# Attention's half-tile moves issued by GpSimd instead of SyncE, and the up weights' sums begun 45 instead of 55 planned microseconds apart

## The chip, the core and the metric

One core of a Trainium2 chip. The metric is the device time of one execution in microseconds (us), the median of several; lower is better. The engines that matter are TensorE (PE, with its weight loads as PEld), VectorE (DVE), ScalarE (ACT), GpSimd (POOL) and SyncE (SP). SP computes nothing; it issues DMAs. ACT and POOL can issue DMAs too, from their own streams of instructions. Every engine executes its stream in order.

## What is computed

One layer on x of 1024 tokens by 1024 features, all in float32: a mixer (attention of 8 heads of 64 features with three dilations, beside 4 mLSTM heads of 128) and a gated feed-forward of width 2816 with a short convolution.

```python
h = h + _hybrid_mixer(_rmsnorm(h, mixer_norm_w[layer]), w_in[layer], ...)
h = h + _conv_ffn(_rmsnorm(h, ffn_norm_w[layer]), w_ffn_up[layer], ...)
return _rmsnorm(h, final_norm_w)

s = jnp.einsum('nbqhd,nbkhd->nbhqk', qb, kk) * (Dh ** -0.5)      # scores of a head
u = _causal_dwconv(h @ w_ffn_up, ffn_conv_w, ffn_conv_b)         # up projection
```

## The kernel before, in words

**Precision by splitting.** Most operands are cut into a high part and a remainder of float32r type, and a product is made of three matmuls (`mm3`). The remainder of a weight tile (`w15l`, `w16l`, ...) is subtracted on POOL or DVE.

**Heads.** The features of x times a head's query and key columns come out of PE as one tile `t`: queries in partitions 0 to 63 (`lo`), keys in 64 to 127 (`up`). `stacks(h, ps)` (line 912) scales it, makes the high part `q1` (`copy`, ACT or DVE) and the remainder `q2` (DVE), and then needs three stacked tiles: `kS` holds the key's remainder over the key's high part, `q1` the query's high part over the query's remainder, `q2` the remainder over the high part. The halves change partitions, so four DMAs of 64 x 1024 floats (256 KB each) move them (lines 931 to 934). The first pair writes `kS` out of `q2` and `q1`. The second pair overwrites the upper halves of `q1` and `q2`, which the first pair has read, so it waits until the first pair has landed. `scores()` (line 943) multiplies `q1` and `q2` with `kS`: 24 matmuls a head, eight heads in order, h0 to h7. In the trace all eight heads' tiles are called `q` and `kS`.

**Sums of weights.** The feed-forward's products use Strassen's seven products in place of eight, for which sums of weight quarters are made in DRAM by `sums` (line 788): a plain copy issued by ACT (line 799), then an add into the same place issued by POOL with `accum_op` (line 796), four times in turn for the up weights (`usum`, 5632 KB each) and four times for the down weights (`tsum`). An add waits until the copy into its place has landed. They stand at lines 804 and 806; the first reader of `usum` is the feed-forward's load, at 589 us in the trace.

**What sets the order.** The program is written out by hand-made lanes (generators), each of which stops at a `yield need(...)`. A planner (`Clock`, line 30) keeps an estimated time for each engine (`clk.eng`), for each tile's readiness (`clk.wr`) and last use (`clk.acc`). `Lanes.run` (line 184) always goes on with the lane of the lowest priority number whose need is met by PE's planned time. So an estimate changes the order of the instructions in the streams, and nothing else: on the chip real semaphores decide. `sums(70, 55, ...)` means: the first step is put into its stream when PE's planned time passes 70, the next at 125, then 180, and so on to 455; odd steps are copies on ACT, even ones adds on POOL. `move` (line 306) issues on SP's queue and advances the planner's `dma` clock. `scores` is put into PE's stream when `q1`, `q2` and `kS` are ready by plan.

**SP's queue.** SP also issues all loads and stores (`dma`, line 291, and `store`, line 1441), in program order with the moves.

Of the kernel before, what the change touches and what calls it, by code (L numbers as in the profile page):

```python
# [217 lines left out]
def need(*tiles, pg=0, bk=0, cond=None, keep=0, kb=0):  # L218

    return tiles, pg, bk, cond, keep, kb  # L220
# [3 lines left out]
def tile_hybrid_layer(ctx, tc, xT, x, w_t, w_v, w_g, w_o, w_uq, w_dq, params, fnw, c_id, c_att, c_sel,  # L224
                      c_rst, c_tri, out):
    nc = tc.nc
    clk = Clock()
# [3 lines left out]
    pool = Engine(clk, nc.gpsimd, "pool")  # L231
# [7 lines left out]
    usum = {p: dram.tile([DFF, 512], F32, name=f"usum{p}") for p in (3, 5, 6, 7)}  # L239
# [8 lines left out]
    def page(name, dt=F32):  # L248
        slot[0] = freep.pop(0)
        t = pages.tile([128, PGW], dt, tag="pg", name=name)  # L250
        clk.floor[t.tensor.name] = slot[0]
        return t

    def free(*ts):
        for t in ts:
            freep.append(clk.last(t))
# [10 lines left out]
    def freebank(t):  # L267
        freeb.append(t)
# [19 lines left out]
    lanes = Lanes(clk, when)  # L288
# [14 lines left out]
    def f32(ap):  # L303
        return ap.bitcast(F32)

    def move(dst, src):

        nc.sync.dma_start(f32(dst), f32(src))
        t = max(clk.eng.get("dma", 1.7), clk.ready(src), clk.last(dst))
        clk.eng["dma"] = t + 0.7  # L310
        for a in (dst, src):
            n = a.tensor.name
            clk.acc[n] = max(clk.acc.get(n, 0.0), clk.eng["dma"] + 2.0)
        for k in clk.cells(dst):
            clk.wr[k] = clk.eng["dma"] + 2.0
            clk.weng[k] = "dma"

    def copy(out_, in_, scale=None):

        if clk.eng.get("act", 0.0) <= clk.eng.get("dve", 0.0):  # L320
            act.activation(out_, in_, AF.Copy, **({} if scale is None else {"scale": scale}))
        elif scale is None:
            dve.tensor_copy(out_, in_)
        else:
            dve.tensor_scalar(out_, in_, scale, None, op0=OP.mult)
# [10 lines left out]
    class Feed:  # L336
# [54 lines left out]
        def put(self, whl):  # L391
            for hi, lo in whl:
                free(hi, lo)
# [11 lines left out]
    for o in order.split():  # L405
        n = int(o[1])
# [171 lines left out]
    def fin_ready(ps, hf):  # L578

        if hf < len(ps) and "R" in flags:  # L580
            return max(clk.ready(ps[hf]), 1e-9)
        return False
# [65 lines left out]
    def project():  # L648

        for n, (kind, arg) in enumerate(plan):  # L650
# [7 lines left out]
            if kind in ("ml", "att"):  # L658
                (wh, wl), = whl
                ps = []  # L660
                for hf in range(2):
                    yield wneed(whl, bk=1, kb=FGB - 1 if "R" in flags else 1)
                    p = bank("fg")
                    if hf == 0:
                        lanes.add(ml_conv(arg, ps) if kind == "ml" else stacks(arg, ps), 3)
                    for k in range(8):
                        ks = slice(k * 128, (k + 1) * 128)
                        mm3(p, wh[:, ks], wl[:, ks], xh[k][:, H[hf]], xl[k][:, H[hf]], k == 0, k == 7)
                        yield need()
                    ps.append(p)  # L670
# [117 lines left out]
    def sums(t, dt, quarters, into, order):  # L788


        flat = lambda a: a.rearrange("(r c) n -> r (c n)", c=4)
        for to, src, add in order:
            yield need(cond=lambda: clk.eng.get("pe", 0.0) > t)
            src = flat(quarters[src] if isinstance(src, tuple) else into[src])
            if add:
                nc.gpsimd.dma_start(flat(into[to]), src, accum_op=OP.add, max_dma_last_dim=8192)
                clk.eng["pool"] = clk.eng.get("pool", 0.0) + 1.5
            else:
                nc.scalar.dma_start(flat(into[to]), src)
            t += dt  # L800

    uq = {(i, j): w_uq[i, j] for i in range(2) for j in range(2)}
    dq = {(i, j): w_dq[i, j] for i in range(2) for j in range(2)}
    lanes.add(sums(70, 55, uq, usum, ((5, (1, 0), 0), (5, (1, 1), 1), (6, 5, 0), (6, (0, 0), 1), (3, 6, 0),
                                      (3, (0, 1), 1), (7, (1, 0), 0), (7, (0, 0), 1))), 0.5)
    lanes.add(sums(530, 45, dq, tsum, ((5, (0, 0), 0), (5, (0, 1), 1), (6, 5, 0), (6, (1, 1), 1), (4, 6, 0),
                                       (4, (1, 0), 1), (7, (0, 1), 0), (7, (1, 1), 1))), 0.6)
# [104 lines left out]
    def stacks(h, ps):  # L912
        for hf in range(2):
            yield need(pg=0 if hf else 4, keep=2, cond=lambda: fin_ready(ps, hf))
            if hf == 0:
                t = page("t")
            dve.tensor_mul(t[:, H[hf]], ps[hf], R[:, H[hf]])
            freebank(ps[hf])
        if h == 7:
            free(R)  # L920
        yield need(t, pg=3)
        q1 = page("q1", F32R)
        q2 = page("q2", F32R)
        kS = page("kS", F32R)
        lo, up = slice(0, 64), slice(64, 128)
        A = slice(0, S)
        copy(q1[:, A], t[:, A])
        yield need(q1)
        dve.tensor_sub(q2[:, A], t[:, A], f32(q1[:, A]))
        yield need(q2)  # L930
        move(kS[lo, A], q2[up, A])
        move(kS[up, A], q1[up, A])
        move(q1[up, A], q2[lo, A])
        move(q2[up, A], q1[lo, A])
        free(t)
        den = small.tile([128, 8], F32, name="aden", bufs=4)
        heads[h] = (q1, q2, kS, den)
# [761 lines left out]
```

## Time and profile before

| what | us |
|---|---|
| median of 3 runs | 1254.02 |
| lowest and highest run | 1248.43, 1255.01 |
| profiled execution, its own time | 1251.1 |
| its span | 1249.3 |
| PE busy | 1221.0 (98%) |
| DVE, ACT, POOL busy | 868.2, 576.5, 300.0 |
| mean granted share of PE's clock | 0.99 |

Busy time says how long an engine had work, not whether it set the end. Here PE is busy nearly all the time, so what counts is the few places where PE waits, what released it, and at which clock it ran.

### The profile page before, as it was taken

What the parts mean: (1) busy time and instruction counts of PE and PEld (TensorE: products, weight loads), DVE (VectorE), ACT (ScalarE), POOL (GpSimd) and SP (SyncE); (2) the same over time, 40 slices, a digit from 0 to 9 for tenths busy, and PEclk for the clock granted to TensorE, in tenths of its full rate; (3) what the DMA queues carried; (4) which work ended last, traced back from release to release, by engine and by line L of the source; (5) the groups of instructions that cost most, each with busy time, mean ns of one, the idle gap of its engine ahead of it and who ended that gap; (6) DMA issues with size and microseconds to landing.
All of it is one profiled execution on the core that took longest, in us unless ns stands there. A gap on an engine that the chain in (4) does not pass through costs nothing. (4 is left out here: it accounts for less than half of the span.)

```text
span 1249.3 us, 17498 instructions
## 1 busy us (share of the span) xinstructions
PE 1221.0 (98%) x6366; PEld 1031.3 (83%) x6366; DVE 868.2 (69%) x1622; ACT 576.5 (46%) x1146; POOL 300.0 (24%) x213
## 2 busy tenths in 40 slices
PE   9999999999999699999999999999999999999997
PEld 6899898988998598788878888888888888888886
DVE  6733472657784487635799877777776878877865
ACT  4454554536562366334654344343343444343553
POOL 3420132121103103121133332323322222424002
PEclk9999999999999799999999999999999999999999
DMA  9460656668493759823663865546634279433334
GB/s 332 174 213 25 147 163 231 144 152 251 129 193 94 269 178 233 214 86 142 143 212 133 243 222 164 188 161 195 179 107 152 82 288 409 148 102 90 97 97 147
DMA packets 66366, 216.41 MB, mean 173 GB/s; under 512 B 7268, under 2 KB 8804, under 8 KB 61288
## 3 DMA queue, kind: packets, MB, share of 16 engines
q1 hardware_dynamic: 61032, 146.09, 34.8%
q0 software_dynamic: 4352, 34.60, 13.7%
q10 hardware_dynamic: 896, 34.60, 8.1%
q8 instruction: 50, 0.82, 0.3%
q14 instruction: 36, 0.29, 0.1%
HBM read 182.76 MB, written 93.32 MB: 221 GB/s over the span
## 5 line engine op out<-in xcount | busy, mean ns | idle before, releaser
L153 PE MATMUL bank<-xb,W 128*128 128x512 f32 x1848 | 431.1, 395 | 2.6 <-POOL W L153 2.1
L153 PEld LDWEIGHTS bank<-xb,W 128*128 128x128 f32 x1848 | 347.8, 188 | 84.9 <-POOL W L153 2.5
L153 PE MATMUL bank<-B,A 128*128 128x512 f32 x924 | 214.0, 394 | 0.0
L153 PEld LDWEIGHTS bank<-B,A 128*128 128x128 f32 x924 | 173.6, 188 | 40.2
L153 POOL TENSOR_TENSOR W<-ur,W 128x512 fp32r<-128x512 f32 x82 | 107.2, 1329 | 278.4 <-ACT W L153 258.0
L153 ACT ACTIVATE ua<-bank,pr 128x512 f32<-128x512 f32 x84 | 63.0, 777 | 168.9 <-DVE bank L153 161.0
L153 DVE SCALAR_TENSOR_TENSOR ua<-bank,pr,ua 128x511 f32<-128x511 f32 (+1 forms) x168 | 125.4, 746 | 15.9 <-ACT ua L153 12.9
L153 DVE TENSOR_TENSOR bank<-bank,ut 128x512 f32<-128x512 f32 x84 | 58.6, 697 | 38.2 <-PE bank L153 37.2
L153 ACT ACTIVATE W<-ur 128x512 fp32r<-128x512 f32 x133 | 78.5, 623 | 5.9 <-DMA ur<-in_w_uq_dram 3.2
L153 ACT ACTIVATE A<-g 128x512 fp32r<-128x512 f32 x76 | 47.3, 627 | 71.9 <-DVE g L153 47.2
L153 DVE CUSTOM_DVE_ANT_0 P<-bank,matt 128x512 f32<-128x512 f32 (+3 forms) x96 | 50.7, 552 | 19.6 <-PE bank L153 17.5
L153 ACT ACTIVATE P<-P,nmx 128x128 f32<-128x128 f32 (+3 forms) x64 | 49.5, 773 | 29.3 <-DVE nmx L153 29.0
L153 DVE TENSOR_TENSOR ut<-ut,bank 128x512 f32<-128x512 f32 x66 | 45.0, 681 | 19.5 <-PE bank L153 19.0
L153 DVE TENSOR_TENSOR B<-br,B 128x512 fp32r<-128x512 f32 x67 | 50.4, 755 | 11.5 <-ACT B L153 11.4
L153 DVE TENSOR_TENSOR PT<-bank,PT 128x512 fp32r<-128x512 f32 (+1 forms) x80 | 48.3, 630 | 8.2 <-ACT PT L153 7.9
L153 PE MATMUL bank<-kS,q 128*128 128x512 f32 (+3 forms) x192 | 42.4, 354 | 10.9 <-DMA q<-q 10.9
L153 POOL TENSOR_TENSOR A<-g,A 128x512 fp32r<-128x512 f32 x17 | 23.2, 1372 | 122.2 <-ACT A L153 122.2
L153 DVE TENSOR_TENSOR W<-ur,W 128x512 fp32r<-128x512 f32 x72 | 49.9, 701 | 2.2 <-ACT W L153 1.5
L153 DVE TENSOR_TENSOR A<-g,A 128x512 fp32r<-128x512 f32 x60 | 41.7, 700 | 13.6 <-ACT A L153 13.2
L153 DVE TENSOR_TENSOR hq<-hq,bank 128x512 f32<-128x512 f32 x56 | 34.9, 681 | 20.9 <-PE bank L153 20.9
L153 ACT ACTIVATE B<-br 128x512 fp32r<-128x512 f32 x69 | 42.4, 619 | 14.9 <-DMA br<-in_w_dq_dram 10.1
L153 ACT ACTIVATE PT<-bank 128x512 fp32r<-128x512 f32 (+1 forms) x71 | 36.5, 547 | 24.9 <-PE bank L153 23.4
(357 smaller groups left out, 2467.2 us busy)
## 6 DMA issues: line engine op xcount, KB each, us to landing
usum<-in_w_uq_dram POOLq DMA_DIRECT2D x4, 5632.0 KB, 34.9
ur<-usum SPq DMA_DIRECT2D x88, 256.0 KB, 4.5
ur<-in_w_uq_dram SPq DMA_DIRECT2D x66, 256.0 KB, 4.6
usum<-in_w_uq_dram ACTq DMA_DIRECT2D x2, 5632.0 KB, 21.1
usum<-usum ACTq DMA_DIRECT2D x2, 5632.0 KB, 22.8
tsum<-in_w_dq_dram POOLq DMA_DIRECT2D x4, 2816.0 KB, 18.1
gp<-ua SPq DMA_DIRECT2D x22, 512.0 KB, 2.9
g<-gp SPq DMA_DIRECT2D x22, 512.0 KB, 7.6
```

The costliest lines, as they stand in the source:

```text
L153: r = f(*a, **k)
```

## The change

The moves go from SP's queue to POOL's: `put` takes the place of `move`, issues by `nc.gpsimd.dma_start`, and advances the planner's `pool` clock by 1.0 a move instead of the `dma` clock by 0.7. The planner counts a move as landed 4.0 after its start (before: 2.7). Between the first pair and the second stands a new `yield need(kS)`: the second pair is put into the stream only when PE's planned time has reached `kS`'s planned landing, and other lanes may go on meanwhile. The steps of the up weights' sums are begun at planned times 70, 115, 160, 205, 250, 295, 340 and 385 instead of 70, 125, 180, 235, 290, 345, 400 and 455. The down weights' sums stay.

```diff
-    def move(dst, src):
-
-        nc.sync.dma_start(f32(dst), f32(src))
-        t = max(clk.eng.get("dma", 1.7), clk.ready(src), clk.last(dst))
-        clk.eng["dma"] = t + 0.7
+    def put(dst, src):
+
+        nc.gpsimd.dma_start(dst, src)
+        t = max(clk.eng.get("pool", 0.0), clk.ready(src), clk.last(dst))
+        clk.eng["pool"] = t + 1.0
         for a in (dst, src):
             n = a.tensor.name
-            clk.acc[n] = max(clk.acc.get(n, 0.0), clk.eng["dma"] + 2.0)
-        for k in clk.cells(dst):
-            clk.wr[k] = clk.eng["dma"] + 2.0
-            clk.weng[k] = "dma"
+            clk.acc[n] = max(clk.acc.get(n, 0.0), t + 4.0)
+        if dst.tensor.name in clk.floor:
+            for k in clk.cells(dst):
+                clk.wr[k] = t + 4.0
+                clk.weng[k] = "dma"
...
-    lanes.add(sums(70, 55, uq, usum, ((5, (1, 0), 0), (5, (1, 1), 1), (6, 5, 0), (6, (0, 0), 1), (3, 6, 0),
+    lanes.add(sums(70, 45, uq, usum, ((5, (1, 0), 0), (5, (1, 1), 1), (6, 5, 0), (6, (0, 0), 1), (3, 6, 0),
                                       (3, (0, 1), 1), (7, (1, 0), 0), (7, (0, 0), 1))), 0.5)
...
-        move(kS[lo, A], q2[up, A])
-        move(kS[up, A], q1[up, A])
-        move(q1[up, A], q2[lo, A])
-        move(q2[up, A], q1[lo, A])
+        put(f32(kS[lo, A]), f32(q2[up, A]))
+        put(f32(kS[up, A]), f32(q1[up, A]))
+        yield need(kS)
+        put(f32(q1[up, A]), f32(q2[lo, A]))
+        put(f32(q2[up, A]), f32(q1[lo, A]))
```

## Rows read from the trace of the kernel before

**Rows 1.** The page: the span, and busy time with its share by engine.
```profile
span 1249.3 us, 17498 instructions
PE 1221.0 (98%) x6366; PEld 1031.3 (83%) x6366; DVE 868.2 (69%) x1622; ACT 576.5 (46%) x1146; POOL 300.0 (24%) x213
```
**Rows 2.** PE's waits, whole span: waiting <- released by: total us, times, longest.
```profile
PE bank L153 <- DMA q<-q: 10.9, 2, 8.9
```
**Rows 3.** Timeline of PE, 410 to 442: start, us, instructions, [idle before <- releaser].
```profile
417.70 1.14 PE L153 MATMUL bank<-kS,q 128*128 128x512 f32 x4
427.74 0.48 PE L153 MATMUL bank<-kS,q 128*128 128x128 f32 x1 [8.89 <-DMA q<-q]
430.22 1.65 PE L153 MATMUL bank<-kS,q 128*128 128x128 f32 x5 [2.00 <-DMA q<-q]
431.67 0.63 PE L153 MATMUL bank<-xh,w17h 128*128 128x512 f32 x1
...
435.34 0.39 PE L153 MATMUL bank<-xl,w17h 128*128 128x512 f32 x1
```
**Rows 4.** Timeline of SP's queue: moves of h2 (first pair), h4 (first), h5 (both).
```profile
312.31 3.75 SPq L308 DMA_DIRECT2D kS<-q x2
...
393.63 1.10 SPq L308 DMA_DIRECT2D kS<-q x2
...
403.54 1.11 SPq L308 DMA_DIRECT2D kS<-q x2
411.53 1.10 SPq L308 DMA_DIRECT2D q<-q x2
```
**Rows 5.** DMA issues at 393, 403 and 411: count, KB each, median us to landing.
```profile
kS<-q SPq DMA_DIRECT2D x2, 256.0 KB, 3.2
kS<-q SPq DMA_DIRECT2D x2, 256.0 KB, 7.3
q<-q SPq DMA_DIRECT2D x2, 256.0 KB, 16.2
```
**Rows 6.** Tile usum: issue ns, first and last start; then landings, issues at 345, 408, 480.
```profile
L796 POOL DMA_DIRECT2D usum<-in_w_uq_dram x4: 1132/1172/1291, 133.4 to 480.4; - x4
L799 ACTq DMA_DIRECT2D usum<-in_w_uq_dram x2: 503/552/602, 72.0 to 408.3; - x2
L799 ACTq DMA_DIRECT2D usum<-usum x2: 477/485/493, 184.9 to 296.9; - x2
...
usum<-in_w_uq_dram POOLq DMA_DIRECT2D x1, 5632.0 KB, 32.1
usum<-in_w_uq_dram ACTq DMA_DIRECT2D x1, 5632.0 KB, 21.0
usum<-in_w_uq_dram POOLq DMA_DIRECT2D x1, 5632.0 KB, 38.8
```
**Rows 7.** DMA queues between 411 and 427: packets, MB, share of 16 engines.
```profile
q10 hardware_dynamic: 115, 5.05, 88.4%
q1 hardware_dynamic: 92, 0.32, 5.4%
```
**Rows 8.** Page: the one queue of DMAs that POOL issues, packets, MB, share.
```profile
q0 software_dynamic: 4352, 34.60, 13.7%
```
**Rows 9.** DMA issues of the first 17 us, queue q1: 64 KB loads, ahead and behind.
```profile
w0r<-in_w_t_dram SPq DMA_DIRECT2D x6, 64.0 KB, 2.3
...
ident<-in_c_id_dram SPq DMA_DIRECT2D x1, 64.0 KB, 5.5
```
**Rows 10.** Timeline of POOL, 376 to 412.
```profile
384.12 2.92 POOL L153 TENSOR_TENSOR adn<-ams,ahp 128x16 f32<-128x16 f32 x1 [4.23 <-DVE ams L153]
387.03 2.42 POOL L153 TENSOR_TENSOR w17l<-wr,w17h 128x1024 fp32r<-128x1024 f32 x1
```
**Rows 11.** Timeline of PE: first score matmuls of h2 and of h4.
```profile
329.92 0.62 PE L153 MATMUL bank<-kS,q 128*128 128x128 f32 x4
...
403.71 1.57 PE L153 MATMUL bank<-kS,q 128*128 128x128 f32 x9
```

## The prediction, made before the changed kernel was run

> **What bounds the kernel now.** I read the page first: PE is busy 1221.0 of 1249.3 us [rows 1], so the end is set by PE, and a change can only move the time through PE's waits, its clock, or the amount of its work. The work doesn't change. The list of PE's waits came next: the only one of any size that a DMA ends is the one on `q<-q`, attention's second pair of moves, 10.9 us in two pieces [rows 2]. No wait of PE for a weight load is in that list, so what stands behind the moves on SP's queue costs nothing today.
>
> The timeline of PE shows the place. The scores of h5 should begin when the matmuls of 417.70 end, at 418.84; they begin at 427.74 and 430.22 [rows 3]. After that idle time a 128x512 matmul takes 0.63 us up to 435 and 0.39 from there on [rows 3], that is PE at the lower of its two clock levels (1.2 GHz) and then at the higher one (2.4). From 430.2 to 435.1 that costs about half of 4.9 us, 2.4 us. So this one stall is worth 10.9 + 2.4 = 13.3 us.
>
> Why it is there: h5's second pair was issued at 411.53 [rows 4] and took 16.2 us to land, where a pair on quiet queues takes 3.2 [rows 5]. A 5632 KB copy for the sums had been issued by ACT at 408.3 and landed 21.0 us later [rows 6]. Between 411 and 427 the copy's queue q10 moved 5.05 MB and SP's queue q1 0.32 [rows 7]. Moves and sums share the DMA engines, and the moves lose.
>
> **The change part by part.**
>
> *The copies go away from h5.* The planned times of the four copies were 70, 180, 290, 400, and they were issued at 72.0, 184.9, 296.9 and 408.3 [rows 6]: planned time plus 2.0, 4.9, 6.9, 8.3. The last copy is now planned at 340, so about 347.5 real, and lands at 347.5 + 21.0 = 368.5. h5's moves (403 to 412) find no copy: the stall of 13.3 us goes. What is late next there is the following part.
>
> *The adds come under the moves.* The adds were planned at 125, 235, 345, 455 and are now at 115, 205, 295, 385. One lasts 32.1 to 38.8 us [rows 6]; I take 35. The old ones were in flight at 133 to 167, 228 to 265, 345 to 377 and 480 to 519, beside no pair of moves but, just, h7's. The new third one runs at about 292 to 337, the new fourth at about 391 to 426. For the fourth: planned 385 is about 393 in real time by the offset above, but POOL can run ahead of PE as far as its own work lets it, and its stream is busy until 387.03 + 2.42 = 389.45 [rows 10]. I take 391, with 380 and 396 as ends. h4's first pair of moves is ready at 393.63 [rows 4].
>
> *The moves join the adds' queue.* All that POOL issues is in one queue, q0: its 34.60 MB are those of the eight adds alone [rows 8]. From now on the moves stand in it behind the adds. No row shows two DMAs in q0 at once, so I bound the wait. Lower bound: q0's DMAs don't hold each other up, and a move takes the 3.2 us of a quiet pair [rows 5]. Upper bound: a move starts when the add ahead of it is through. The nearest row for order inside one queue is q1 at the start: a 64 KB load lands 2.3 us after issue, and one of the same size issued behind half a megabyte and more of other loads of that queue 5.5 us after [rows 9]. That is the nearer kin, so I take the upper bound. The Trainium skill says the same in words: on its page "DMA: Bandwidth & Descriptors", section "Queues, rings and completion order", each engine consumes the descriptors of one ring in order, while different rings take turns by packet; and by the section "SWDGE vs HWDGE vs iDMA" only one queue is allocated for DMAs issued by GpSimd. By that rule moves behind an add wait for all of it; the trace of before shows neither for q0.
>
> *The price for h4.* The add issued at 391 lands at 426. h4's first pair lands with it, at about 426.5. POOL then issues the second pair: an add's issue costs POOL 1.13 to 1.29 us [rows 6], a move's on SP 0.55 (1.10 for two [rows 4]); I take 1.0 each, so 2. Landing takes 3.2 to 3.5 more: `q1` and `q2` are ready at 432. PE reaches h4's scores at 403.71 in the trace of before [rows 11]; the planner now counts about 10 us for the four moves instead of 6.8, so it fills in some 3 us of other matmuls first: 407. Stall: 432 - 407 = 25 us. After it the clock is low for about as long as in rows 3, 2.4 us. Sum +27.4. With the add issued at 380 and landing in 32.1 it is 412 + 5.5 - 407 = 11 us; with 396 and 38.8 it is 33 us. It hardly matters on which side of h4's first pair the add falls in POOL's stream: if the add comes between the pairs, the second pair waits for it instead, and h4 is ready at 396 + 35 + 1 = 432 again. If it comes behind all four, h5's moves of 403.54 wait in its place.
>
> *h2.* The third add, issued between 291 (when POOL has issued h1's moves) and 302, lands between 326 and 337. h2's first pair (312.31 [rows 4]) lands then, its second 5.5 us later, at 331.5 to 342.5. h2's scores begin at 329.92 [rows 11] and now about 333: between 0 and 9.5 us, I take 2, since POOL tends to be early. h3, h0, h1 have either slack or no add beside them: 0.
>
> *POOL's own time.* 32 issues at 1.0 us are 32 us on an engine that is busy 300.0 of 1249.3 [rows 1]. Behind a waiting second pair stand weight remainders (like `w17l`, 2.42 us [rows 10]) and the small `adn`. They are made one unit ahead of use, and between 250 and 520 us PE's list of waits has none on them; I take 0, and up to 3 us if h4's wait holds one up that isn't covered by PE's own stall.
>
> *SP freed.* SP no longer stops at moves; loads are issued earlier. PE waits for none of them: 0.
>
> *Sum*, against the profiled execution's 1251.1 us: -13.3 + 27.4 + 2 = +16.1, 1267. That execution lies 2.9 below the median of the runs, 1254.0; on the median the sum gives 1270. I forecast 1269.
>
> **The rivals.**
>
> *Moves aren't held behind an add (faster).* If q0 lets a move through in its usual time, or if the order shifts so that the moves of h4 and h5 fall outside the adds, the old stall is gone and nothing replaces it: -13.3, 1241. It decides at one point: whether a move issued during an add lands in some 3 to 6 us or with the add. For it: no row contradicts it, and packets of two different queues do mix in the trace (q1 moved its 0.32 MB beside q10 [rows 7]). Against it: rows 9, and that the two windows of 10 to 12 planned us of h4 and h5 both lie within 35 us of planned 385, so a dodge needs a shift of the plan of over 20 us. Chance 0.25.
>
> *One stall for another (no change).* The stall of h4 comes out at about 13 us and only replaces h5's: the add must have landed by about 414, thus been issued by 379 to 382. POOL would have to issue it ahead of `adn`, for which it waits 4.23 us before 384.12 [rows 10]; that is possible if the planner sets it there. Time 1250 to 1258. Chance 0.10.
>
> *The forecast, slower.* 1259 to 1282, chance 0.65.
>
> **How the numbers follow.** Over 0.5%, about what a measurement of this kernel can tell from no change, is 6.3 us. Slower 0.65, same 0.10, faster 0.25. The slower case's own range is 1259 (stall 15) to 1282 (stall 33, h2 5). To leave out no more than 2 in 10 the range must reach into the faster case: I take 1240 to 1282, which leaves out about half of that case and the tail above.
>
> **What would show it.** In the profile after: PE's waits should have a stall of 20 to 30 us on the moves (`DMA q<-q` or `kS`) once, near 407 to 432, with PE's clock at 1.2 GHz behind it; the stall at 418 to 430 should be gone; moves issued by POOL during an add should show a landing time of 15 to 35 us, others 3 to 5; POOL should wait long for `kS<-q` in front of a second pair. If moves during an add land within 6 us, the queue step is wrong and the time will be near 1241. If no add is in flight when h4's and h5's moves go, the planned offsets were wrong. If a stall is there but PE waits for a `w..l` tile, POOL's queue was the price.

## The result, and the profile after

The changed kernel takes 1272.88 us (median of 4 runs, 1270.92 to 1273.61) beside 1251.94 of the kernel before on the same chip: 1.0166 times as long, 95% interval 1.0132 to 1.0200. The forecast was 1269, slower.

The page of the profile after. The answers to [rows 1] and [rows 8]:

```profile
span 1271.8 us, 17500 instructions
PE 1221.9 (96%) x6366; PEld 1032.0 (81%) x6366; DVE 865.1 (68%) x1616; ACT 580.4 (46%) x1152; POOL 315.7 (25%) x245
...
q0 software_dynamic: 6912, 42.99, 16.2%
```

PE's busy time is nearly the same, 1221.9 us over as many instructions; the 22.5 us that the span grew are PE's waiting and its lower clock. q0 grew from 34.60 to 42.99 MB: the 32 moves joined the eight adds. PE's waits, the answer to [rows 2] (waiting <- released by: total us, times, longest):

```profile
PE bank L153 <- DMA q<-q: 34.5, 4, 17.5
PE bank L153 <- POOL W L153: 2.0, 1, 2.0
```

The wait on the moves grew from 10.9 to 34.5 us. The timeline of PE shows it at two places, and none at h5 any more (the answer to [rows 3]):

```profile
321.74 0.62 PE L153 MATMUL bank<-kS,q 128*128 128x512 f32 x2
339.55 0.44 PE L153 MATMUL bank<-kS,q 128*128 128x128 f32 x1 [15.55 <-DMA q<-q]
340.75 2.50 PE L153 MATMUL bank<-kS,q 128*128 128x128 f32 x7 [0.75 <-DMA q<-q]
...
448.84 0.45 PE L153 MATMUL bank<-kS,q 128*128 128x128 f32 x1 [17.49 <-DMA q<-q]
450.01 0.98 PE L153 MATMUL bank<-kS,q 128*128 128x128 f32 x3 [0.72 <-DMA q<-q]
```

The first is h2 (16.3 us), the second h4 (18.2 us). The timeline of POOL tells why, the answer to [rows 4] and [rows 10]:

```profile
300.22 1.06 POOL L308 DMA_DIRECT2D q<-q  x2
301.27 1.23 POOL L797 DMA_DIRECT2D usum<-in_w_uq_dram  x1
302.01 1.54 POOL L308 DMA_DIRECT2D kS<-q  x2
336.58 1.02 POOL L308 DMA_DIRECT2D q<-q  x2 [33.02 <-issue]
...
413.17 1.11 POOL L308 DMA_DIRECT2D kS<-q  x2 [4.58 <-issue]
414.27 1.23 POOL L797 DMA_DIRECT2D usum<-in_w_uq_dram  x1
...
419.75 1.50 POOL L308 DMA_DIRECT2D q<-q  x2
```

Around 301 the third add goes out right ahead of h2's first pair, and POOL then sits idle for 33 us before it issues the second pair ("issue" says that the profile names no releaser; the first pair, for which it must wait, has landed at 335.5 by the rows below). Around 414 the fourth add falls between h4's two pairs. The landing times, the answer to [rows 5] and [rows 6], of what was issued between 300 and 303, then at 413, then at 419 (count, KB, median us to landing):

```profile
usum<-in_w_uq_dram POOLq DMA_DIRECT2D x1, 5632.0 KB, 33.6
q<-q POOLq DMA_DIRECT2D x2, 256.0 KB, 3.5
kS<-q POOLq DMA_DIRECT2D x2, 256.0 KB, 33.5
...
kS<-q POOLq DMA_DIRECT2D x2, 256.0 KB, 3.2
...
q<-q POOLq DMA_DIRECT2D x2, 256.0 KB, 29.3
```

Moves issued one us ahead of an add land in 3.5 and 3.2 us, as on SP before. Moves issued behind it land in 33.5 and 29.3, with the add. What the DMA engines did meanwhile says whether the moves were slow or not begun. All packets between 306 and 326, then the table of queues there, then all packets between 336 and 338, when h2's second pair of moves runs alone:

```profile
DMA packets 513, 4.21 MB, mean 211 GB/s; under 512 B 0, under 2 KB 0, under 8 KB 0
...
q0 software_dynamic: 512, 4.19, 102.0%
...
DMA packets 22, 0.09 MB, mean 45 GB/s; under 512 B 0, under 2 KB 0, under 8 KB 22
```

A move's packets are smaller than 8 KB. In these 20 of the 33 us for which h2's first pair stood in q0 behind the add, not one packet under 8 KB was moved. The pair was not slow, it had not begun.

### The profile page after: what moved, and what is told of

Read it like the earlier page. It is cut to its first block, busy times and chain, and to the rows that moved or that the text cites. A ratio compares the mean times of both kernels' runs of the same rounds, so it can differ in the third digit from the quotient of the medians.

```text
span 1271.8 us, 17500 instructions
## 1 busy us (share of the span) xinstructions
PE 1221.9 (96%) x6366; PEld 1032.0 (81%) x6366; DVE 865.1 (68%) x1616; ACT 580.4 (46%) x1152; POOL 315.7 (25%) x245
## 3 DMA queue, kind: packets, MB, share of 16 engines
q0 software_dynamic: 6912, 42.99, 16.2%
q10 hardware_dynamic: 896, 34.60, 8.2%
## 5 line engine op out<-in xcount | busy, mean ns | idle before, releaser
L153 DVE SCALAR_TENSOR_TENSOR ua<-bank,pr,ua 128x511 f32<-128x511 f32 (+1 forms) x168 | 125.3, 746 | 16.1 <-ACT ua L153 12.9
L153 DVE TENSOR_TENSOR bank<-bank,ut 128x512 f32<-128x512 f32 x84 | 58.5, 697 | 30.0 <-PE bank L153 28.8
L153 PE MATMUL bank<-kS,q 128*128 128x512 f32 (+3 forms) x192 | 43.1, 357 | 34.5 <-DMA q<-q 34.5
L153 PEld LDWEIGHTS bank<-kS,q 128*128 128x128 f32 x192 | 32.8, 197 | 39.0 <-issue 34.7
L153 DVE TENSOR_TENSOR W<-ur,W 128x512 fp32r<-128x512 f32 x72 | 50.0, 701 | 13.8 <-ACT W L153 13.2
L153 ACT ACTIVATE B<-br 128x512 fp32r<-128x512 f32 x69 | 42.4, 620 | 16.0 <-DMA br<-in_w_dq_dram 11.1
```

Of the source, the lines that this page charges most:

```text
L153: r = f(*a, **k)
```

## The experiments

Three theories were kept apart. **A**: a move waits in GpSimd's queue until the add ahead of it is through. **B**: the adds take the DMA engines, so a move beside an add is slow in any queue. **C**: the new order of the streams, the later second pair or the issue by GpSimd costs the time by itself. Ratios are against the kernel before on the same chip.

| run | what | us (median) | ratio, 95% interval |
|---|---|---|---|
| sp_queue | changed, moves issued by SP | 1260.13 | 1.0073, 1.0049 to 1.0097 |
| moves_only | changed, sums 55 apart | 1248.90 | 0.9979, 0.9960 to 0.9998 |
| sums_only | before, sums 45 apart | 1280.54 | 1.0233, 1.0200 to 1.0266 |
| no_second_wait | changed, without the new wait | 1264.82 | 1.0110, 1.0079 to 1.0140 |
| no_late_adds | changed, third and fourth add left out | 1239.07 | 0.9900, 0.9877 to 0.9923 |
| chunked | changed, adds in quarters | 1238.89 | 0.9903, 0.9878 to 0.9928 |
| early_pool | changed, sums from 40 on, 30 apart | 1244.37 | 0.9941, 0.9917 to 0.9964 |
| early | before, sums from 40 on, 30 apart | 1240.08 | 0.9909, 0.9888 to 0.9929 |
| chunked_sp | chunked, moves issued by SP | 1249.99 | 0.9977, 0.9960 to 0.9994 |

### Is it the queue: the same streams with the moves on SP (sp_queue)

```diff
-        nc.gpsimd.dma_start(dst, src)
+        nc.sync.dma_start(dst, src)
```

> The changed kernel with one word other: the moves go out on SP's queue again, with the planner told the same as in the changed kernel, so that the streams of PE, DVE and ACT are those of the changed kernel instruction by instruction. Theory A (a move waits in GpSimd's queue until the add ahead of it is through): the two stalls of 16 and 18 us on q<-q go, moves issued while an add is in flight land in 4 to 10 us, and the time is 1236 to 1248. Rival B (the add slows the moves by taking the DMA engines, whatever queue they are in): stalls of over 25 us in sum stay, 1265 to 1273. Rival C (the new order of the streams or the new wait is the price): the streams are the same, so 1265 to 1275.

Measured 1260.13: 12.8 us less than the changed kernel, but 12 over what A gave and 5 under B's range. By the traces every engine computes the same instructions in the same order as in the changed kernel. h2 is the clean comparison, since its add and its moves are issued at nearly the same times as there, 300.6 and 301.9. Landing times of what was issued between 301 and 303, and between 314 and 316, and PE at h2's scores:

```profile
kS<-q SPq DMA_DIRECT2D x2, 256.0 KB, 10.7
...
q<-q SPq DMA_DIRECT2D x2, 256.0 KB, 9.7
...
326.65 1.44 PE L153 MATMUL bank<-kS,q 128*128 128x128 f32 x7 [2.23 <-DMA q<-q]
```

Beside the same add, in another queue, the pair takes 10.7 us instead of 33.5, and h2's stall shrinks from 16.3 to 2.2. So the queue is what made h2 wait. But 10 us is three times the 3.2 of [rows 5]: B is right as well, in a smaller measure. And SP's queue has an order of its own: six loads of `w_o` now go out between h4's pairs, and all of it runs beside the fourth add. PE's timeline and the landing of those loads and of h4's second pair:

```profile
424.68 0.79 PE L153 MATMUL bank<-xh,w18h 128*128 128x512 f32 x1 [10.30 <-ACT w18h L153]
429.47 0.80 PE L153 MATMUL bank<-xh,w18l 128*128 128x512 f32 x1 [3.57 <-POOL w18l L153]
435.37 0.45 PE L153 MATMUL bank<-kS,q 128*128 128x128 f32 x1 [5.10 <-DMA q<-q]
...
wr<-in_w_o_dram SPq DMA_DIRECT2D x6, 512.0 KB, 30.7
...
q<-q SPq DMA_DIRECT2D x2, 256.0 KB, 27.5
```

The second pair lands in 27.5 us behind six loads that take 30.7. PE's first wait there is for `w18h`, and ACT's stream had the splitting of a late `w_o` load (`w0h`, a wait of 20.7 us) ahead of it. PE's waits in these rows, with one of 0.8 us behind them, sum to 19.8 us. It is the add that makes the loads late: the same six take 7.1 us in the changed kernel, where they go out at 394.6, ahead of its fourth add, and 10.6 in chunked_sp below, where the adds are in quarters. So the fourth add still costs some 20 us here, by another way.

### Each part alone (moves_only, sums_only)

```diff
-    lanes.add(sums(70, 45, uq, ...
+    lanes.add(sums(70, 55, uq, ...
```

> The changed kernel with the sums begun 55 planned us apart as before: the moves' change alone. In GpSimd's stream the third add stands behind all moves of h3 and the fourth behind all of h7. Theory A: no move has an add ahead of it, so no stall behind an add; the copy planned at 400 can still meet h4's or h5's moves as in the kernel before (0 to 13 us): 1238 to 1256. Rival B: adds are in flight beside fewer moves, so also 1240 to 1258. Rival C (issuing from GpSimd or the new wait costs the time by itself): 1265 to 1275.

Measured 1248.90, 0.2% under the kernel before. C falls: issuing by GpSimd with the later second pair costs nothing that the total shows. The waits on moves sum to 11.5 us, much as in [rows 2], and the larger part, 8.1, is again beside a copy: the copy issued by ACT at 298.1 catches h1's second pair, issued at 302.3. The other 3.4 us are at h5:

```profile
PE bank L153 <- DMA q<-q: 11.5, 4, 6.8
...
q<-q POOLq DMA_DIRECT2D x2, 256.0 KB, 17.1
```

The sums alone, moves on SP as before:

```diff
-    lanes.add(sums(70, 55, uq, ...
+    lanes.add(sums(70, 45, uq, ...
```

> The kernel before with the sums begun 45 planned us apart, moves on SP: the sums' change alone. Theory A: the moves of h2, h4 and h5 run beside adds in another queue and land in 4 to 10 us, and no copy meets h5: the stall of 13.3 us of the kernel before goes, 1236 to 1246. Rival B: the adds under the moves of h2, h4 and h5 give stalls of 20 to 35 us, 1258 to 1275. Rival C: 1236 to 1252.

Measured 1280.54, the slowest of all, where A gave 1236 to 1246. A is wrong in this: a queue without the adds doesn't protect the moves. PE's waits on the moves, then SP's queue and its landing times in this run, with the third add issued at 281.8:

```profile
PE bank L153 <- DMA q<-q: 33.0, 6, 10.9
...
285.21 0.62 SPq L902 DMA_DIRECT2D parked<-yh  x1
285.92 0.48 SPq L902 DMA_DIRECT2D parked<-yl  x1
286.50 0.41 SPq L292 DMA_DIRECT2D wr<-in_w_t_dram  x1
287.01 1.33 SPq L308 DMA_DIRECT2D kS<-q  x2
...
parked<-yl SPq DMA_DIRECT2D x1, 512.0 KB, 24.3
wr<-in_w_t_dram SPq DMA_DIRECT2D x1, 512.0 KB, 30.5
kS<-q SPq DMA_DIRECT2D x2, 256.0 KB, 32.4
```

h1's first pair stands behind two stores and a load of 512 KB each; beside the add that queue crawls, the stores and the load land some 7 us after one another, and the pair is through after 32.4. The waits on moves sum to 33.0 us, about as much as in the changed kernel: 7.6 at h0 and 11.7 at h1 beside the third add, 13.8 at h4 beside the fourth. So the two parts of the change are these: the sums' new times cost 28.8 us alone (1251.71 to 1280.54), the moves' new queue gains 2.8 alone and 7.7 on top of the sums' (1280.54 to 1272.88).

### The second pair's place (no_second_wait)

```diff
-        yield need(kS)
```

> The changed kernel without the new wait between the two pairs: all four moves of a head stand together in GpSimd's stream. The third add stands right ahead of h2's four moves, the fourth right ahead of h4's. Theory A: both pairs wait for the add, so the stalls stay at 15 to 30 us each, 1268 to 1290. Rival C (the later second pair is the price): 1245 to 1258.

Measured 1264.82, a little under the range of A and over that of C. The stalls are there, 5.7 us at h2 and 18.8 at h4, with the adds ahead of both pairs:

```profile
PE bank L153 <- DMA q<-q: 24.5, 4, 17.8
```

h2's is smaller because PE comes to h2's scores 7 us later in this order (330.8 instead of 324.0) and h2's tiles are ready 4 us sooner (337.0 instead of 340.75). The place of the second pair is not the cause of the stalls; with what it shifts in the streams it is worth 8 us.

### Taking the adds away (no_late_adds)

```diff
-                nc.gpsimd.dma_start(flat(into[to]), src, accum_op=OP.add, max_dma_last_dim=8192)
+                if t not in (295, 385):
+                    nc.gpsimd.dma_start(flat(into[to]), src, accum_op=OP.add, max_dma_last_dim=8192)
```

> The changed kernel with the third and the fourth add of the up weights' sums left out (planned 295 and 385; the planner is told the same, so the streams of the other engines stay; two of the four sums miss an addend). Theory A (moves wait in GpSimd's queue behind the adds): with no add in the queue both stalls go. They cost 16.3 and 18.2 us of waiting and some 2.5 us each at the lower clock, 39.5 in sum: 1272.9 - 39.5 = 1233, with 1232 to 1240. Rival C (the order of the streams, the later second pair or the issue by GpSimd costs the time): 1262 to 1273.

Measured 1239.07, near the upper end of A's range, and far under C's. Every engine computes the same instructions in the same order as in the changed kernel, so with the streams as they were the two adds are worth 33.8 us. PE's list has no wait on moves left; its longest are these:

```profile
PE bank L153 <- DMA ymh<-parked: 2.8, 2, 2.0
PE bank L153 <- POOL W L153: 2.0, 1, 2.0
```

### Smaller adds, and adds out of the way (chunked, chunked_sp, early_pool, early)

In `sums`, each add in four pieces (chunked):

```diff
-                nc.gpsimd.dma_start(flat(into[to]), src, accum_op=OP.add, max_dma_last_dim=8192)
-                clk.eng["pool"] = clk.eng.get("pool", 0.0) + 1.5
+                n = src.shape[0] // 4
+                for c in range(4):
+                    yield need(cond=lambda: clk.eng.get("pe", 0.0) > t + 10 * c)
+                    rs_ = slice(c * n, (c + 1) * n)
+                    nc.gpsimd.dma_start(flat(into[to])[rs_], src[rs_], accum_op=OP.add, max_dma_last_dim=8192)
+                    clk.eng["pool"] = clk.eng.get("pool", 0.0) + 0.8
```

> The changed kernel with every add issued in four quarters, 10 planned us apart (those of the down weights too). Theory A: a move then has at most one or two quarters of about 8 to 9 us ahead of it, not 34, and the other moves slip in between: stalls of 0 to 10 us at h2 and at h4, 1236 to 1255. Rival B (the adds' traffic slows the moves in whatever queue): the same traffic is spread over the same time, stalls as before, 1262 to 1275.

Measured 1238.89: all bytes are added, in the same queue and over much the same stretch, and 34 us are back. PE's order differs a little from the changed kernel's, from 323 us on; but that kernel's own order, in no_late_adds, gives the same time once its two late adds are away, so the order is not what the 34 us come from. The run beats both kernels. The wait on moves is nearly gone; the landing times between 380 and 425, where the quarters and h4's and h5's moves meet:

```profile
PE bank L153 <- DMA q<-q: 2.4, 2, 2.2
...
usum<-in_w_uq_dram POOLq DMA_DIRECT2D x4, 1408.0 KB, 15.9
kS<-q POOLq DMA_DIRECT2D x4, 256.0 KB, 4.8
q<-q POOLq DMA_DIRECT2D x4, 256.0 KB, 12.1
```

A move waits for a quarter or two: the second pairs take 12.1 us in the median of four moves, 8.7 at h4 and 14.8 at h5, and all but 2.4 us of that fits into the slack that the planner leaves. chunked_sp is the same kernel with `nc.sync.dma_start` in `put`.

> The kernel with adds in quarters (run chunked, 1238.9 us) with the moves on SP's queue again; the streams of PE, DVE and ACT are the same instruction by instruction. With whole adds the move to SP's queue gained 12.8 us (1272.9 to 1260.1). Theory A (what SP's queue gained was not standing behind a whole add; SP's queue has a price of its own, the loads that stand ahead of the moves and behind them): with quarters there is little left to gain and the price stays, 1238 to 1256, not faster than with the moves on GpSimd. If GpSimd's queue is still the price with quarters: 1228 to 1235.

Measured 1249.99, inside A's range and 11 us slower than chunked (9 by the ratios in the table), with 11.0 us of waits on moves. With whole adds SP's queue was the better by 12.8 us, with quarters GpSimd's is the better by 11.1. So GpSimd's queue is not bad in itself; a long transfer ahead of the moves in it is.

The two kernels with the sums begun ahead of the heads (early has the same edit on the line of the kernel before, `sums(70, 55, ...`):

```diff
-    lanes.add(sums(70, 45, uq, ...
+    lanes.add(sums(40, 30, uq, ...
```

> The changed kernel with the sums begun at planned 40, 70, 100, ... 250: the last add stands in GpSimd's stream ahead of h0's moves and should land before or shortly after them. Theory A: no move has an add or a copy ahead of it or beside it, no stall in attention: 1234 to 1243, below both kernels. A new wait is possible: ACT may reach a copy before the add that it reads has landed (30 planned us against 33 to 38), which can cost up to 10 us in the mLSTM stage: 1243 to 1252 then. Rival C: 1258 to 1270.

> The kernel before with the sums begun at planned 40, 70, ... 250, moves on SP. Theory A: as with the moves on GpSimd, the queue no longer matters once the sums are through: 1234 to 1245; if ACT waits for adds, up to 1252. Rival C (GpSimd's issue is the price): faster than the same sums with moves on GpSimd by 10 us or more.

Measured 1244.37 and 1240.08. The first is 1.4 us over A's first range: the last add, issued at 258.4, lands after 34.5 us, h0's first pair stands behind it from 276.7 on and lands after 18.8, and PE waits 8.1 us for h0. The second is inside. There too the last add still runs beside h0's first pair, which lands after 11.6 us on SP's queue, and PE waits 4.9. PE's waits on moves in the two:

```profile
PE bank L153 <- DMA q<-q: 8.1, 2, 7.1
...
PE bank L153 <- DMA q<-q: 4.9, 2, 3.5
```

So where one head alone meets an add, the two queues differ by 3.2 us of these waits. The run early tells one thing more. By the traces every engine computes the same instructions in the same order in the kernel before, in sums_only and in early, and SP issues the same DMAs in the same order; what differs is when the copies and the adds are issued, and that alone takes the time from 0.9909 to 1.0233 of the kernel before.

## Why the prediction was right, point by point

**The copies go away from h5, -13.3.** Right: no wait at h5 in the profile after, and its 13.3 us of [rows 2, 3] are gone. h5's first pair, issued at 424.67 behind the fourth add, lands after 25.8 us, while PE still stands at h4. The fourth copy was issued at 367.9, not 347.5, mostly because PE had stalled 16.3 us at h2 by then: in no_late_adds, without that stall, it goes out at 349.8.

**The moves join the adds' queue and wait for all of it.** Right, and this was the step for which the trace before had no row. The upper bound was the right end: 33.5 and 29.3 us to landing, and no packet of the moves in the 20 us looked at. The rule cited from the Trainium skill, page "DMA: Bandwidth & Descriptors", section "Queues, rings and completion order", that the descriptors of one ring are consumed in order, agrees with these rows.

**h4, +27.4.** The mechanism as described, in the variant with the add between the two pairs. Size: 18.2 us of waiting and 4.9 us at the lower clock after it, which cost half of that (2.45): +20.7. Ready 36.8 us after its first pair was issued (413.17 to 450.01), forecast 38.4; but PE came to h4's scores 18.2 us after that issue, not 13.4, so the planner had put more other matmuls first than I counted.

**h2, +2.** This is the term that was mis-sized: 16.3 us of waiting and 2.5 of lower clock, +18.8, twice the upper end of 9.5. The add (301.27) and the second pair's landing (340.75) are inside the ends given (291 to 302, 331.5 to 342.5). What failed is the time at which PE needs h2: I carried over 329.92 [rows 11] plus 3. In the changed streams h2's first pair is ready at 302.0, ten us sooner than [rows 4], and PE stands at h2's scores at 324.0. A change of the planner's estimates moved the order itself, and I let it move only by the added estimate. That is 9.0 of the 16.8 us by which the term was too small; 5.3 come from taking 2 out of a range that went to 9.5, and 2.5 from the lower clock behind the stall, which I counted at h4 and not here.

**The sum.** With measured terms: -13.3 + 18.8 + 20.7 = 26.2. From the kernel before also go a gap of 1.28 at 475 and one of 1.97 at 514 with 1.7 of lower clock behind it; two gaps of 1.28 in all come at 471. 26.2 - 4.95 + 1.28 = 22.5, the growth of the span. The forecast's +16.1 was near because h4 was taken too dear by 6.7 and h2 too cheap by 16.8. So the sum's nearness is in part luck: two errors of opposite sign. Right by its mechanism and its sign, less so by its terms. The sign that was named, one stall of 20 to 30 us, came as two, of 16.3 and 18.2.

The clock behaves the same in all three stalls. Stretches of the changed kernel (length, busy us of PE, PEld, DVE, ACT, POOL with instructions, granted clock, DMA share, GB/s):

```profile
340.70:345.70 5.00, 4.95 (x20) 4.76 (x21) 3.63 (x14) 1.61 (x4) 0.20 (x1) 0.50 0.00 0
345.70:350.00 4.30, 4.30 (x39) 4.30 (x38) 2.35 (x4) 4.28 (x12) 2.18 (x1) 1.00 0.02 6
...
450.00:454.90 4.90, 4.89 (x14) 3.92 (x15) 2.22 (x7) 1.10 (x4) 1.52 (x4) 0.50 0.22 53
```

After the idle time PE works for some 5 us at a granted clock of 0.50 (1.2 GHz) before it is back at 1.00 (2.4 GHz), here as in [rows 3].

**POOL's own time, 0.** Right, and the issue was cheaper than taken: 1.02 to 1.15 us for a pair in most rows, not 2. **SP freed, 0.** Right but for the 1.28 us at 471, where PE waits for reloads of `parked` by SP; why these come late no run shows. **The rival "moves aren't held behind an add"** gave 1241, with a move landing in 3 to 6 us during an add. The run in which no move stands behind an add is sp_queue: 1260.13, with h2's moves landing in 9.7 to 10.7 us. So the lower bound of 3.2 us was too low, and taking the moves out of the adds' queue gives back 12.8 us, not the 28 between the forecast and the rival. What comes near 1241 are the runs without the two adds (1239.07), with all adds in quarters (1238.89) and with the sums begun early (1244.37 and 1240.08). **What I didn't see**: that the adds under the moves hurt on SP too (sums_only). The argument put all the price on the queue; the runs put it on the adds' new times first (28.8 us alone), with the queue deciding how it is paid.

## What to carry to other kernels

A short transfer on which a busy engine waits should not be issued into a queue in which long ones are started: look in the trace for what will be in flight there at that time, and take its full landing time as the longest that the short one can wait for it. Before moving a transfer to another queue, count what it will stand behind in each of the two, loads and stores as well; cutting the long transfer into pieces (34 us) or running it earlier (28.5 with the moves on GpSimd) helped more here than the choice of queue (12.8). And when a planner's estimates change, don't carry over the time at which an engine needs something: the order moves too.

## What the runs showed that was not expected

A pair of moves of 256 KB each takes 3.2 us on quiet queues, 9.7 to 10.7 beside a 5632 KB add in another queue (sp_queue, h2), 16.2 beside a 5632 KB plain copy [rows 5], and up to 33.5 behind an add in its own. The plain copy, which lands in 21 us, left its neighbour less while it ran (q1 moved 0.32 MB beside 5.05 in 16 us [rows 7]) than the add, which takes 33.6 (q1 moved 0.86 MB beside 2.84 of q0 in the 16 us from 396 in sp_queue). In another queue beside an add, loads fare badly too: six of 512 KB took 30.7 us in the median, and 7.1 with no add beside them. And quartering an add doesn't quarter its landing time: 15.9 us in the median beside the moves, and 12.8 for the one issued at 327.8 with nothing ahead of it in its queue, against 33.6 for the whole.
